# State-space set-up in two parts, one plain pair, and complex products in three passes, in a Trainium2 encoder block

## The chip, the core and the metric

The kernel runs on one core of one Trainium2 chip. Five engines work side by side: PE (TensorE, matrix products; PEld is its weight load), DVE (VectorE), ACT (ScalarE), POOL (GpSimd) and SP (SyncE, which here issues nearly all DMAs, in one queue and in order). Each engine runs its own instructions in order and waits on semaphores of the others. The metric is the time of one execution in microseconds (us), the median of several runs. Arithmetic is float32; a matrix product is built of three matmuls, since each operand is split into a high and a low fp32r part (high x high, high x low, low x high).

## The reference, cut to what matters

```python
h = rms_norm(x, g_ffn1_pre)
x = x + 0.5 * rms_norm(swiglu(h, w_gate, w_up, w_down), g_ffn1_post)   # FFN 1
z = rms_norm(x, g_mix_pre) @ w_in             # -> u | q_c | kv_c | k_rope
y_ssm = rms_norm(s5_mixer(u, fwd, bwd, d_skip, w_glu, b_glu), g_ssm_out)
y_att = rms_norm(mla_mixer(q_c, kv_c, k_rope, ...), g_att_out)
x = x + rms_norm(concat(y_ssm, y_att) @ w_out, g_mix_post)
x = x + 0.5 * rms_norm(swiglu(rms_norm(x, g_ffn2_pre), ...), g_ffn2_post)   # FFN 2

def ssm_direction(u_c, lam_re, lam_im, log_dt, b_re, b_im, c_re, c_im, reverse):
    lam = complex(lam_re, lam_im); dt = exp(log_dt)
    lam_bar = exp(lam * dt)                        # 32 groups x 64 states
    b_bar = ((lam_bar - 1) / lam) * b              # 64 states x 16 channels
    s = linear_recurrence(lam_bar, b_bar @ u_c)    # forwards or backwards in time
    return real(c @ s)
```

x is 512 + 256 = 768 tokens of 1024 channels, D_FF is 2816, there are 32 groups of 16 channels and 8 heads. One layer is computed.

## The kernel before

The stages follow one another on PE: FFN 1, its **way out** (post-norm, residual, pre-norm and transposes into the operand of the next stage), the **mixer** (state-space part and attention), its way out, FFN 2, its way out.

**The FFN** (`ffn`, both times the same function) goes over D_FF in 11 **pairs** of 128 columns, and over the tokens in halves of 384. A **plain** pair takes gate and up as 16 products of 12 matmuls of 128x384; a **Winograd** pair (`wino`) takes 14 such products and some additions of weights on DVE, and needs the combinations T1 to T4 of the activations. T1 to T4 are built once by `combos`, beside the down product of the last plain pair. The down product of a pair (`down`) is 12 products of six matmuls of 128x512, added into `acc` on DVE. Each weight tile is loaded by SP, cast on ACT (line 98) and its remainder taken on DVE (line 99). FFN 1 is called with n_plain = 3 and FFN 2 with n_plain = 1: line 1186 passes 3 for FFN 1, and FFN 2 (the call below it) passes 1. FFN 2 has nothing in the background.

**The state-space set-up** (`ssm_setup`) computes from the parameters alone what the mixer needs: the powers of lam_bar, and for 16 blocks of two groups the matrices W (discretised b times powers) and CL (c times powers). Each complex product is six real passes (`cmul`, lines 517 to 522): W on POOL with 128x256 elements a pass, CL on DVE with 128x320. Per block PE transposes W (`ps_m`, line 668), takes the eight small matmuls of the local kernel (`ps_k`, line 682), and SP writes dM, dO and dK to DRAM (lines 671, 673, 690). The generator is woven into FFN 1 by `behind(steps, PACE)`: after each half product it takes PACE steps of it and ties what these issue behind the last traced instruction of each engine. At `q == n_plain - 1` the rest of it is drained, ahead of `combos`, so the whole of the set-up lies in the three plain pairs.

**The mixer** (`mix`): projection of u; inputs of the state recurrence (`ps_x` from dM, copied into XS); then the **recurrence** on POOL, 62 steps of four dependent instructions each (lines 782 to 785); beside it on PE the projections of q, kv, rope (`rot`, lines 871 and 876) and of the heads. The rotated parts of q go through 16 DMAs into qT (line 878). Attention begins with `ps_s` (line 948). When the recurrence has ended, ACT reverses one direction (line 1017), and `ps_y` (line 1030) takes XS, dO and dK (as T).

**What sets the order.** The code is traced, and a list scheduler then sets the order of each engine from a modelled timeline, the traced order and these ties. Tiles come from pools by tag, with N6 = 18 slots for the wide s6, N4 = 15 for w4 (weights) and N2 = 4 for t2; a tile waits until its slot is free.

## Time and profile before

| what | us |
|---|---|
| median of 3 runs (1502.71 to 1505.95) | 1504.83 |
| the profiled execution | 1503.25 |
| its span | 1501.5 |
| FFN 1, first product to the last | 18.51 to 569.06 |
| of it plain pairs 0 to 2 with the down products and combos | to 254.56 |
| way out of FFN 1 | 569.06 to 616.5 |
| mixer, with its way out | to 976.19 |
| of it recurrence on POOL | 695.77 to 818.69 |
| FFN 2, first product to the last | 976.19 to 1459.35 |

The stages are cut by the first and last matmul of a kind on PE in the trace. PE is busy for 95% of the span; the mean granted clock of PE is 0.979 of full speed. The execution had one core, whose span is the time but for 1.75 us around it.

### The profile page before, as it was taken

Reading aid. Unit: us, or ns where it says so; the run is one execution under the profiler, and the core shown is the slowest. Engines: PE = TensorE matmul, PEld = TensorE weight load, DVE = VectorE, ACT = ScalarE, POOL = GpSimd, SP = SyncE. Lnnn points to the kernel's source line nnn. Section 1 sums busy time; section 2 is a strip of 40 time slices with the busy share of each in tenths; the row PEclk is TensorE's granted clock in tenths of the full one; section 3 lists DMA queues with packets and bytes.
Section 4 is the critical chain, followed back from the end, with each engine's and each line's share of the span. In section 5 each row is a group of like instructions: output and inputs, shape, how many; then the busy total and the mean of one; then the engine's idle time right before and its main releaser. Section 6 shows DMA issues by size and latency. Waiting matters only on the chain. (4 is left out here: it accounts for less than half of the span.)

```text
span 1501.5 us, 20634 instructions
## 1 busy us (share of the span) xinstructions
PE 1427.0 (95%) x7868; PEld 1304.6 (87%) x7868; DVE 1004.7 (67%) x1616; ACT 580.1 (39%) x1101; POOL 347.7 (23%) x525
## 2 busy tenths in 40 slices
PE   6988979999999999899998999799999999999996
PEld 6977858999999997799976988598999999999995
DVE  5596898677766676714265445797777667776664
ACT  5233333233322243424765654346343223332231
POOL 1368740000000003305997112532000000000004
PEclk9999999999999999899999999999999999999999
DMA  8323312212121224462104433322122212212124
GB/s 243 83 73 124 123 60 82 74 58 83 57 84 57 71 87 138 142 191 85 42 1 128 139 100 141 126 99 85 57 71 71 84 57 71 71 57 84 58 97 112
DMA packets 116355, 137.53 MB, mean 92 GB/s; under 512 B 32032, under 2 KB 96928, under 8 KB 116256
## 3 DMA queue, kind: packets, MB, share of 16 engines
q1 hardware_dynamic: 116256, 136.21, 29.7%
q8 instruction: 62, 1.02, 0.3%
q14 instruction: 37, 0.30, 0.1%
HBM read 113.44 MB, written 21.95 MB: 90 GB/s over the span
## 5 line engine op out<-in xcount | busy, mean ns | idle before, releaser
L98 ACT CAST w<-raw 128x512 fp32r<-128x512 f32 (+3 forms) x327 | 219.9, 692 | 297.2 <-PE ps_d L126 88.0
L99 DVE TENSOR_TENSOR w<-raw,w 128x512 fp32r<-128x512 f32 (+3 forms) x327 | 256.0, 799 | 61.2 <-ACT w L98 53.0
L453 DVE TENSOR_TENSOR acc<-acc,ps_d 128x512 f32<-128x512 f32 x216 | 145.9, 683 | 119.2 <-PE ps_d L127 119.0
L125 PE MATMUL ps_d<-w,hid 128*128 128x512 f32 x528 | 210.3, 399 | 7.0 <-DVE acc L453 4.4
L126 PE MATMUL ps_d<-w,hid 128*128 128x512 f32 x528 | 209.5, 397 | 0.0
L127 PE MATMUL ps_d<-w,hid 128*128 128x512 f32 x528 | 207.1, 396 | 0.0
L1146 POOL TENSOR_SCALAR g<-g 128x1024 f32<-128x1024 f32 x2 | 5.6, 2780 | 754.5 <-DMA g<-in_g_ffn_post 419.5
L125 PEld LDWEIGHTS ps_d<-w,hid 128*128 128x128 f32 x528 | 100.3, 190 | 27.2 <-DVE acc L453 5.3
L127 PEld LDWEIGHTS ps_d<-w,hid 128*128 128x128 f32 x528 | 100.4, 190 | 21.8
L126 PEld LDWEIGHTS ps_d<-w,hid 128*128 128x128 f32 x528 | 100.5, 190 | 16.9
L400 ACT COPY U<-pa 128x384 f32<-128x384 f32 x36 | 17.3, 480 | 151.7 <-PE pa L119 143.8
L98 ACT CAST hid<-hs 128x384 fp32r<-128x384 f32 x88 | 44.4, 512 | 74.6 <-DVE hs L348 73.8
L99 DVE TENSOR_TENSOR hid<-hs,hid 128x384 fp32r<-128x384 f32 x88 | 47.9, 557 | 5.4 <-ACT hid L98 5.3
L117 PE MATMUL pe<-T1h,w 128*128 128x384 f32 x144 | 48.8, 339 | 1.8 <-DVE acc L453 1.8
L951 DVE TENSOR_REDUCE mx<-ps_s 128x1 f32<-128x512 f32 (+1 forms) x40 | 27.2, 686 | 32.8 <-PE ps_s L948 32.7
L119 PE MATMUL pe<-T1h,w 128*128 128x384 f32 x144 | 48.9, 339 | 0.0
L118 PE MATMUL pe<-T1l,w 128*128 128x384 f32 x144 | 48.8, 339 | 0.0
L344 ACT ACTIVATE hs<-hs 128x384 f32<-128x384 f32 x54 | 28.3, 526 | 52.1 <-DVE hs L430 39.3
L119 PE MATMUL pa<-B00h,w 128*128 128x384 f32 x144 | 48.4, 336 | 0.0
L117 PE MATMUL pe<-B11h,w 128*128 128x384 f32 x144 | 48.3, 336 | 0.0
L118 PE MATMUL pa<-B00l,w 128*128 128x384 f32 x144 | 48.3, 335 | 0.0
L119 PE MATMUL pe<-B11h,w 128*128 128x384 f32 x144 | 48.3, 335 | 0.0
(372 smaller groups left out, 3893.9 us busy)
## 6 DMA issues: line engine op xcount, KB each, us to landing
raw<-in_w_ffn_gate SPq DMA_DIRECT2D x44, 512.0 KB, 3.7
raw<-in_w_ffn_up SPq DMA_DIRECT2D x44, 512.0 KB, 4.1
raw<-in_w_ffn_down SPq DMA_DIRECT2D x44, 512.0 KB, 3.6
x<-in_x_prompt SPq DMA_DIRECT2D x16, 256.0 KB, 7.4
dO<-ssm_w SPq DMA_DIRECT2D x32, 128.0 KB, 2.1
dM<-ssm_stg SPq DMA_DIRECT2D x16, 256.0 KB, 2.1
raw<-dM SPq DMA_DIRECT2D x8, 512.0 KB, 7.0
raw<-dO SPq DMA_DIRECT2D x8, 512.0 KB, 3.8
```

The source lines that it names most:

```text
L98: self.nc.scalar.copy(hi, src)
L99: (eng or self.nc.vector).tensor_tensor(lo, src, hi.bitcast(F32), op=ALU.subtract)
L117: self.nc.tensor.matmul(ps, A[0][:, k, :], B[0][:, k, :], start=first, stop=False, skip_group_check=True)
L118: self.nc.tensor.matmul(ps, A[0][:, k, :], B[1][:, k, :], start=False, stop=False, skip_group_check=True)
L119: self.nc.tensor.matmul(ps, A[1][:, k, :], B[0][:, k, :], start=False, stop=stop and k == 3, skip_group_check=True)
L125: self.nc.tensor.matmul(ps, lh, rh, start=i == 0, stop=False)
L126: self.nc.tensor.matmul(ps, lh, rl, start=False, stop=False)
L127: self.nc.tensor.matmul(ps, ll, rh, start=False, stop=last)
L344: nc.scalar.activation(hs[:, i, half(nh)], ps, AF.Silu)
L400: nc.scalar.copy(U2, pa)
L453: tt(acc[:, t, sl], acc[:, t, sl], ps, op=ALU.add)
L951: nc.vector.tensor_reduce(m, ps, axis=AX.X, op=ALU.max)
```

## The change

1. FFN 1 is called with n_plain = 1 in place of 3: pairs 1 and 2 become Winograd pairs, and `combos` runs beside the down product of pair 0.
2. `ssm_setup` computes only the front part: powers, W, `ps_m`, dM. It goes behind the halves of pair 0 with 2.0 steps each and behind the down products of pairs 1 to 10 with 0.3 steps each, and is drained ahead of the last two pairs' down product. Two small results go to DRAM, dB (discretised b) and dP (powers).
3. A new `ssm_back` computes CL, `ps_k`, dO and dK in the mixer. It loads dP and, per block, a piece of dB. It is woven behind the projections of q and kv (KPACE = 1.1 steps) and of rope and heads (2.2 steps), and is drained ahead of the first load of dK.
4. Complex products are three passes on DVE (`product`): the two halves of one operand stand side by side, with the signs already in the other operand, so that a pass covers real and imaginary part: 128x512 elements for W, 128x576 for CL. POOL makes none any more.
5. N6 becomes 20 and N2 becomes 6; a scratch size for DMA descriptors is set to 1024.

The diff, cut to its core:

```diff
-PACE = 1.9
+PACE = (2.0, 0.3)
+KPACE = 1.1
...
-    N6, N4, N2 = 18, 15, 4
+    N6, N4, N2 = 20, 15, 6
...
                         if q or nh:
-                            self.behind(background, PACE)
+                            self.behind(background, PACE[0])
...
                 for dh in range(2):
                     product(t, dh, self.dn)()
                     if side is background:
-                        self.behind(side, PACE)
+                        self.behind(side, PACE[1])
...
                 if q == n_plain - 1:
-                    for _ in background:
-                        pass
                     self.free = True
...
                 load_m("u", q + 1)
+        for _ in background:
+            pass
         acc, product = row_of([Q - 1, Q])
...
+        W = {}
+        for b in range(17):
+            if b < 16:
+                W[b] = self.t2("ssm_w", [512])
+                self.product(W[b], self.t2("ssm_t", [512]), Bm, QW, 2 * b, 8)
+                yield
+            if b:
+                ps, w = self.bg([128, 4, 128], "ps_m"), W.pop(b - 1)
+                for x in range(4):
+                    nc.tensor.transpose(ps[:, x, :], w[:, 128 * x : 128 * x + 128], self.ident)
+                stg = self.t2("ssm_stg", [4, 128])
+                nc.scalar.copy(stg, ps)
+                dma(self.dM[:, 2 * b - 2 : 2 * b].rearrange("p g r n -> p (g r) n"), stg)
+                yield
+
+    def product(self, out, tmp, a, b, g0, n):
+        tt = self.nc.vector.tensor_tensor
+        wide = [128, 4, n, 16]
+        a = a[:, g0 : g0 + 2].rearrange("p g r c -> p (g r) c")[:, :, None, :].broadcast_to(wide)
+        b0, b1 = (z[:, g0 : g0 + 2].rearrange("p g r i -> p (g r) i")[:, :, :, None].broadcast_to(wide) for z in b)
+        to = lambda z: z.rearrange("p (x i c) -> p x i c", x=4, c=16)
+        tt(to(out), a, b0, op=ALU.mult)
+        tt(tmp.rearrange("p (g r n) -> p g r n", g=2, r=2)[:, :, ::-1, :], a, b1, op=ALU.mult)
+        tt(out, out, tmp, op=ALU.add)
...
         def matrices(b):
...
+            t = self.s6("ssm_w", [1488])
...
+            dma(v["fB"], self.dB[:, :, 32 * b : 32 * b + 48])
+            self.product(t[:, :576], t[:, 576:1152], CT, PX, 2 * b, 9)
             return v
...
+        back = self.ssm_back()
...
         for nh in range(2):
             for i in range(3):
                 from_h(w_q[i], i, nh, q_done)
+                self.behind(back, KPACE)
...
             proj(wq, slice(512 + 128 * x, 640 + 128 * x), qcT, turned)
+            self.behind(back, 2 * KPACE)
             steps(1)
...
+        for _ in back:
+            pass
 
         kf = self.dK.rearrange("(g q) x -> g q x", q=32)
...
-            way = self.ffn(bl1, (...), out1, 3, feed(), 1, self.ssm_setup(), read)
+            way = self.ffn(bl1, (...), out1, 1, feed(), 1, self.ssm_setup(), read)
```

**SP in FFN 1, the first weight loads after the start.** L69 (L70 after) loads weights (`raw`, of gate, up and down), L671, L673 and L690 write dM, dO and dK from the staging tiles; after, L638 and L649 write dB and dP, L663 dM. Before:

```order
L69 DMA raw<-in_w_ffn_down 128x1024 x2
L673 DMA dO<-ssm_w 128x2x128 x2
L671 DMA dM<-ssm_stg 128x512
L690 DMA dK<-ssm_w 64x240
L671 DMA dM<-ssm_stg 128x512
L673 DMA dO<-ssm_w 128x2x128 x2
L69 DMA raw<-in_w_ffn_gate 128x4x256
L690 DMA dK<-ssm_w 64x240
L673 DMA dO<-ssm_w 128x2x128 x2
L671 DMA dM<-ssm_stg 128x512
L690 DMA dK<-ssm_w 64x240
L671 DMA dM<-ssm_stg 128x512
```

After:

```order
L70 DMA raw<-in_w_ffn_down 128x1024 x2
L70 DMA raw<-in_w_ffn_gate 128x4x256 x2
L638 DMA dB<-ssm_b 128x1056
L649 DMA dP<-ssm_d 128x1152
L663 DMA dM<-ssm_stg 128x512
L70 DMA raw<-in_w_ffn_up 128x4x256 x2
L70 DMA raw<-in_w_ffn_down 128x1024 x2
L70 DMA raw<-in_w_ffn_gate 128x4x256 x2
L663 DMA dM<-ssm_stg 128x512 x2
L70 DMA raw<-in_w_ffn_up 128x4x256 x2
L70 DMA raw<-in_w_ffn_down 128x1024 x2
L70 DMA raw<-in_w_ffn_gate 128x4x256 x2
```

Before, single gate loads stand among the writes of the blocks; after, the loads stand in sixes in the order gate, up, down, with dB, dP and one or two writes of dM between them.

**DVE in the mixer, around the rope products.** L833 to L836 make the latent kv and the rotated key, L841 and L99 split operands, L871 (L913 after) forms the products `rot`; after, L673, L675 and L676 are the three passes of a CL product, L727 and L730 finish a local kernel. Before:

```order
L871 TENSOR_TENSOR rot<-ps,raw 128x384 x2
L833 SCALAR_TENSOR_TENSOR kv<-ps_kv,r,g_kv 128x256
L834 TENSOR_TENSOR kpe<-ps_kv,ropek 128x32
L835 TENSOR_TENSOR kv<-ps_kv,ropek 128x32
L99 TENSOR_TENSOR w<-raw,w 128x8x2x64
L841 TENSOR_TENSOR kvT<-ps_t,kvT 128x128
L871 TENSOR_TENSOR rot<-ps,raw 128x384
L836 TENSOR_TENSOR kpe<-kpe,kv 128x32
L871 TENSOR_TENSOR rot<-ps,raw 128x384
L841 TENSOR_TENSOR kvT<-ps_t,kvT 128x128
L871 TENSOR_TENSOR rot<-ps,raw 128x384 x4
```

After:

```order
L882 TENSOR_TENSOR kvT<-ps_t,kvT 128x128 x2
L673 TENSOR_TENSOR ssm_w<-ssm_b,ssm_d 128x576
L675 TENSOR_TENSOR ssm_w<-ssm_b,ssm_d 128x2x2x144
L727 SCALAR_TENSOR_TENSOR ssm_w<-mask,dsk,ssm_w 64x16
L676 TENSOR_TENSOR ssm_w<-ssm_w 128x576
L730 TENSOR_TENSOR ssm_w<-ssm_w,ps_k 64x16
L913 TENSOR_TENSOR rot<-ps,raw 128x384 x6
L673 TENSOR_TENSOR ssm_w<-ssm_b,ssm_d 128x576
L675 TENSOR_TENSOR ssm_w<-ssm_b,ssm_d 128x2x2x144
L673 TENSOR_TENSOR ssm_w<-ssm_b,ssm_d 128x576
L675 TENSOR_TENSOR ssm_w<-ssm_b,ssm_d 128x2x2x144
L913 TENSOR_TENSOR rot<-ps,raw 128x384 x2
L673 TENSOR_TENSOR ssm_w<-ssm_b,ssm_d 128x576
```

Of the 48 passes of CL, 8 stand ahead of the last copy into XS, and 40 behind it; 26 of these 40 stand ahead of the last `rot<-ps`, 14 behind it.

**POOL in the mixer, around the rotation.** `rec_a`, `rec_b` and XS are the steps of the recurrence, `r` and `rq` norm factors. Before:

```order
L782 TENSOR_TENSOR rec_a<-XS,lam_74 128x128
L783 TENSOR_TENSOR rec_b<-XS,lam_74 128x128
L784 TENSOR_TENSOR rec_a<-rec_a,XS 128x128
L876 TENSOR_TENSOR rot<-rot 128x768 x2
L785 TENSOR_TENSOR XS<-rec_a,rec_b 128x64x2
L170 TENSOR_TENSOR rq<-rq,mhalf 128x6
```

After:

```order
L823 TENSOR_TENSOR rec_b<-XS,lam_76 128x128
L155 TENSOR_TENSOR r<-r,mhalf 128x1
L824 TENSOR_TENSOR rec_a<-rec_a,XS 128x128
L919 TENSOR_TENSOR rot<-rot 128x768
L825 TENSOR_TENSOR XS<-rec_a,rec_b 128x64x2
L822 TENSOR_TENSOR rec_a<-XS,lam_76 128x128
L823 TENSOR_TENSOR rec_b<-XS,lam_76 128x128
L919 TENSOR_TENSOR rot<-rot 128x768
L824 TENSOR_TENSOR rec_a<-rec_a,XS 128x128
```

Both `rot<-rot`, on which the DMAs into qT hang, stood together in the 11th step of the recurrence; they stand now in the 25th and the 26th. On PE, all 16 groups of eight `ps_k` (of which the trace has two records each) stand after the change between `ps_x` and the first `ps_s`; of the 16 groups of four `ps_m`, 9 stand ahead of the last product of FFN 1's gate and up, and 7 in its last down products.

## Rows read from the trace of the kernel before

**Rows 1.** The page: the span, and the busy time of each engine.

```profile
span 1501.5 us, 20634 instructions
PE 1427.0 (95%) x7868; PEld 1304.6 (87%) x7868; DVE 1004.7 (67%) x1616; ACT 580.1 (39%) x1101; POOL 347.7 (23%) x525
```

**Rows 2.** Stretches: us, then PE, PEld, DVE, ACT, POOL busy (count), clock, DMA share, GB/s.

```profile
18.50:569.06 550.56, 530.39 (x2933) 485.91 (x2933) 414.25 (x702) 185.99 (x343) 120.58 (x127) 0.98 0.29 87
18.50:57.80 39.30, 38.80 (x219) 38.00 (x219) 22.58 (x40) 19.31 (x35) 7.64 (x7) 1.00 0.64 167
57.80:254.56 196.76, 177.09 (x1051) 152.26 (x1049) 165.12 (x289) 59.21 (x120) 110.16 (x119) 0.94 0.29 91
300.32:346.08 45.76, 45.76 (x241) 42.68 (x241) 32.65 (x55) 14.70 (x26) 0.00 (x0) 1.00 0.22 69
976.19:1012.90 36.71, 36.71 (x210) 36.64 (x209) 34.48 (x33) 15.25 (x26) 13.41 (x9) 0.95 0.30 101
976.19:1459.35 483.16, 480.89 (x2548) 451.92 (x2547) 354.08 (x548) 174.95 (x302) 24.00 (x12) 1.00 0.23 75
569.06:616.50 47.44, 38.54 (x167) 31.11 (x167) 32.98 (x32) 14.54 (x27) 22.26 (x23) 0.91 0.38 118
```

**Rows 3.** PE timeline in a Winograd pair (start, us): first matmuls of two products.

```profile
302.40 0.33 PE L117 MATMUL pc<-T3h,w 128*128 128x384 f32 x1
...
304.48 0.33 PE L117 MATMUL pd<-T4h,w 128*128 128x384 f32 x1
```

**Rows 4.** Groups by line and form, PE, 18.5 to 569.06: busy us, mean ns, idle before.

```profile
L682 PE MATMUL ps_k<-ssm_w 64*32 64x128 f32 x256 | 19.3, 296 | 10.8 <-DVE ssm_w L689 5.9 <-ACT ssm_stg L670 4.5 <-ACT ssm_w L685 0.4
L668 PE MATMUL ps_m<-ident,ssm_w 128*128 128x128 f32 x64 | 11.6, 311 | 2.4 <-DVE ssm_w L689 2.4
```

**Rows 5.** Groups by line and form, DVE, 18.5 to 569.06: busy us, mean ns, idle before.

```profile
L99 DVE TENSOR_TENSOR w<-raw,w 128x512 fp32r<-128x512 f32 x121 | 84.2, 714 | 17.9 <-ACT w L98 16.9
```

**Rows 6.** Waits of DVE: us in total, times, longest us.

```profile
DVE s L395 <- DMA raw<-in_w_ffn_up: 22.0, 15, 2.4
```

**Rows 7.** Stretches of the mixer, columns as in rows 2.

```profile
690.00:732.00 42.00, 42.00 (x289) 41.83 (x288) 17.85 (x55) 18.51 (x50) 36.93 (x68) 1.00 0.26 74
732.00:750.40 18.40, 17.64 (x93) 15.74 (x92) 0.00 (x0) 16.83 (x31) 16.99 (x37) 1.00 0.13 27
750.40:814.00 63.60, 62.90 (x394) 47.00 (x393) 40.51 (x88) 38.53 (x86) 57.71 (x162) 1.00 0.23 59
```

**Rows 8.** Timeline of all engines in the mixer, 716.9 to 721.

```profile
717.04 0.50 POOL L782 TENSOR_TENSOR rec_a<-XS,lam 128x128 f32<-128x128 f32 x1
...
717.16 1.47 DVE L99 TENSOR_TENSOR w<-raw,w 128x1024 fp32r<-128x1024 f32 x1
...
717.50 1.48 POOL L783 TENSOR_TENSOR rec_b<-XS,lam 128x128 f32<-128x128 f32 x1
...
719.45 0.54 DVE L871 TENSOR_TENSOR rot<-ps,raw 128x384 f32<-128x384 f32 x1
...
719.55 0.47 POOL L785 TENSOR_TENSOR XS<-rec_a,rec_b 128x128 f32<-128x128 f32 x1
```

**Rows 9.** Timeline in FFN 1, DVE and POOL: POOL's pass beside DVE, and alone.

```profile
111.41 0.91 DVE L522 TENSOR_TENSOR ssm_w<-ssm_w,ssm_t 128x320 f32<-128x320 f32 x1
...
111.93 0.86 POOL L517 TENSOR_TENSOR ssm_t<-ssm_q,ssm_a 128x256 f32<-128x256 f32 x1
...
116.41 0.62 POOL L518 TENSOR_TENSOR ssm_w<-ssm_q,ssm_a 128x256 f32<-128x256 f32 x1
```

**Rows 10.** PE timeline: the first scores of attention.

```profile
750.37 1.88 PE L948 MATMUL ps_s<-kT,qT 96*128 96x512 f32 x4
```

**Rows 11.** ACT timeline: the reversal when the recurrence has ended.

```profile
818.72 1.99 ACT L1017 COPY rev<-XS 64x1024 f32<-64x1024 f32 x2 [4.87 <-POOL XS L785]
```

**Rows 12.** PE timeline: the first product that takes the recurrence's states.

```profile
820.80 1.17 PE L1030 MATMUL ps_y<-XS,raw 128*128 128x96 f32 x4 [4.96 <-DVE XS L1019]
```

**Rows 13.** SP timeline: the DMAs of the rotated parts into qT.

```profile
726.29 11.39 SPq L878 DMA_DIRECT2D qT<-rot  x16
```

More of the change, by code (lines that the diff above doesn't have):

```diff
@@ L624, in ssm_setup @@
-        for x in range(2):
-            nc.vector.memset(PX[x], 0.0)
-            nc.vector.tensor_copy(PX[x][0:64, :, 0:9].rearrange("p g i -> p i g"), PW[0:64, x])
-            nc.vector.tensor_copy(PX[x][64:128, :, 1:10].rearrange("p g i -> p i g"), PW[64:128, x, ::-1, :])
-        yield
+        for h, order in ((slice(0, 64), slice(None, None, -1)), (slice(64, 128), slice(None))):
+            for r in range(2):
+                for x, sign in ((0, 1.0), (1, 2.0 * r - 1)):
+                    ts(QW[x][h, :, r, :].rearrange("p g i -> p i g"), q[x][h, order, :], sign, None, op0=ALU.mult)
@@ new lines, in ssm_setup @@
+        yield
+        tB, tD = self.s6("ssm_b", [2, 528]), self.s6("ssm_d", [1152])
+        fx = new("fx", 4).rearrange("p (x r) g -> p x g r", x=2)
+        for r in range(2):
+            ts(fx[:, 0, :, r], fr, 1.0, None, op0=ALU.mult)
+            ts(fx[:, 1, :, r], fi, 2.0 * r - 1, None, op0=ALU.mult)
+        fB, fT = (z.rearrange("p r (g c) -> p g r c", c=16) for z in (tB[:, :, :512], tD[:, :1024].rearrange("p (r x) -> p r x", r=2)))
+        spread = [fx[:, x, :, :, None].broadcast_to([128, 32, 2, 16]) for x in range(2)]
@@ new lines, in ssm_setup @@
+        nc.vector.memset(tB[:, :, 512:], 0.0)
+        tt(fB, Bm, spread[0], op=ALU.mult)
+        tt(fT[:, :, ::-1, :], Bm, spread[1], op=ALU.mult)
+        tt(fB, fB, fT, op=ALU.add)
+        dma(self.dB, tB)
+        yield
+        tD = self.s6("ssm_d", [1152])
+        PX = [tD[:, 576 * x : 576 * x + 576].rearrange("p (g r i) -> p g r i", g=32, r=2) for x in range(2)]
+        for x in range(2):
+            for r in range(2):
+                sign = -1.0 if x and r else 1.0
+                ts(PX[x][0:64, :, r, :].rearrange("p g i -> p i g"), PW[0:64, x], sign, None, op0=ALU.mult)
+                ts(PX[x][64:128, :, r, :].rearrange("p g i -> p i g"), PW[64:128, x, ::-1, :], sign, None, op0=ALU.mult)
+            yield
@@ L632, in ssm_setup @@
                 dma(craw[:, ri, :, s], A[f"c_{p}_{d}"][0].rearrange("(b g) c p -> (g c) b p", b=4))
-            ps = self.bg([128, 4, 128], "ps_c")
-            for b in range(4):
-                nc.tensor.transpose(ps[:, b, :], craw[:, ri, b, :], self.ident)
-            nc.scalar.copy(CT[:, ri], ps.rearrange("p b x -> p (b x)"))
         dsk = self.small.tile([64, 16], F32, name="dsk")
@@ L663, in inputs @@
-        def inputs(v):
-            g0 = 2 * v["b"]
-            ps = self.bg([128, 2, 2, 128], "ps_m")
-            for g in range(2):
-                for x in range(2):
-                    nc.tensor.transpose(ps[:, g, x, :], v["W"][:, x, 128 * g : 128 * g + 128], self.ident)
-            stg = self.t2("ssm_stg", [2, 2, 128])
-            nc.scalar.copy(stg, ps)
-            dma(self.dM[:, g0 : g0 + 2], stg)
-            for x in range(2):
-                dma(self.dO[:, g0 : g0 + 2, x, :], v["CL"][:, x, :, 1:9, :].rearrange("p g i c -> p g (i c)"))
+        for ri in range(2):
+            ps = self.bg([128, 4, 128], "ps_c")
+            for b in range(4):
+                nc.tensor.transpose(ps[:, b, :], craw[:, ri, b, :], self.ident)
+            nc.scalar.copy(CT[:, :, ri, :], ps.rearrange("p b (g c) -> p (b g) c", c=16))
@@ L692, in ssm_setup @@
         ready = []
-        for b in range(18):
+        for b in range(17):
             if b < 16:
                 ready.append(matrices(b))
-            yield
-            if b >= 2:
+            if b:
                 v = ready.pop(0)
-                inputs(v)
-                yield
+                outputs(v)
                 kernels(v, 0)
@@ L841, in mix @@
                 tt(kvT[x][:, 1, tok(t)], pt[:, x, :], kvT[x][:, 0, tok(t)].bitcast(F32), op=ALU.subtract)
+            self.behind(back, KPACE)
             steps(1)
@@ L887, in mix @@
             proj(wq, slice(128 * p, 128 * p + 128), qcT, two_heads(qT[p]))
+            self.behind(back, 2 * KPACE)
             steps(1)
```

64 lines of the change are left out of this document (31 added, 33 removed).

## The prediction, made before the changed kernel was run

> **What bounds the kernel now.** I read the page first: PE is busy for 95% of the span [rows 1], so a change can only bring what PE does not do, what it does slowly, or what others make it wait for. Then the table of stretches, stage by stage, because an average over stages hides that. In FFN 1 PE is busy 530.39 of 550.56 us; of the 20.2 us of idle time 19.7 lie between 57.8 and 254.56, in the two plain pairs that carry the set-up, where the clock is 0.94 too and POOL and DVE work for 110 and 165 us [rows 2]. A Winograd pair behind them takes 45.76 us with PE busy throughout at clock 1.00, DVE at 32.65 us [rows 2]. FFN 2 is the same function with one plain pair and no background: 483.16 us, against 550.56 for FFN 1 [rows 2]. So this kernel has already run FFN 1's new program, without the set-up, in 67.4 us less.
>
> The mixer is bound twice. PE is full until attention starts at 750.37 and through attention [rows 7, 10]. POOL's recurrence, begun at 695.77, ends only after it: ACT waits 4.87 us for the last XS and takes it at 818.72, and PE idles 4.96 us before the first product with it, at 820.80 [rows 11, 12]. POOL's chain ends last, by 5 us.
>
> **The change part by part.** All sums are made against the profiled execution, 1503.25 us; the median is 1.6 us more.
>
> *FFN 1.* Pairs 1 and 2 have 14 products where they had 16. Twelve matmuls take 304.48 - 302.40 = 2.08 us [rows 3], so two pairs give 4 x 2.08 = 8.3 us. Out of FFN 1 go `ps_k` (128 matmuls, two records each), 19.3 us of PE and 10.8 us of idle time before them [rows 4], and with them the cover of two pairs in which everything waited on everything. I don't add these up: FFN 2's time contains them all. New FFN 1 = 483.16 (rows 2), + 2.6, since pair 0 began more slowly here (39.30 against 36.71, rows 2), + 9 groups of `ps_m` at 11.6/16 = 0.73 us each [rows 4] = 6.6, + about 3 for places where the set-up holds a load or a slot back. That is 495.4, or **-55 us**. The front's DVE work, 16 products of three passes of 128x512, costs 0.71 us a pass [rows 5], 34 us, or 3.4 us a pair, and a pair leaves DVE 13.1 us free [rows 2]: hidden. POOL has nothing in a steady pair, so nothing locks there. The 3 us are a choice. Its bounds: nothing at all, with the `ps_m` falling where PE waits anyway (-65), and 2.4 us for each of ten pairs, DVE's longest wait for a weight of an up half [rows 6], in place of the 3 (-34). I take 3 because in the order the weight loads stand in regular sixes with one or two dM between them, and each dM waits for one ACT copy.
>
> *Way out.* Seven groups of `ps_m` stand in the last down products, where PE has no other wait: 7 x 0.73 = **+5** [rows 4]. Not below 0, and at most this, as PE idles 8.9 us of that stretch later on [rows 2].
>
> *Mixer, PE.* 19.3 us of `ps_k` [rows 4] and 1.2 of `ps_c` come in ahead of attention, where PE is full: attention can't begin before 771, and PE would come to `ps_y` 20.5 us later, 5 of which it waited anyway [rows 12]: +15.5.
>
> *Mixer, POOL.* 40 of CL's 48 passes lie beside the recurrence. DVE has room: 17.85 of 42 us, then nothing for 18.4 us [rows 7]. What they do to POOL is in a row: a DVE pass with two SBUF inputs (`w<-raw`, 128x1024, 1.47 us) makes the POOL instruction issued into it take 1.48 us, where the one before took 0.50; a DVE pass with one input in PSUM (`rot<-ps`) leaves POOL its 0.47 [rows 8]. So 0.98 us lost for 1024 elements, and 0.55 for a pass of 576: 40 x 0.55 = 22 us. The smaller price is in FFN 1, 0.86 against 0.62 beside passes of 320 elements [rows 9]: 0.24, 0.43 at 576, 17 us in all. I take the first, since the row stands in this very loop. Two us more for a later start (8 passes stand ahead of the last copy into XS): the recurrence ends at 842.7 and `ps_y` comes at 844.8, **+24**.
>
> The Trainium skill ("SBUF — State Buffer", Who interferes with whom) says that such a pair excludes each other for the whole instruction, whoever issues first. The trace agrees in rows 8 and not in rows 9, where POOL slowed by 0.24 and did not stop; the rival below has what the rule would make of the time.
>
> *Mixer, attention.* Both `rot<-rot` move from POOL's 11th step to the 25th and 26th, and the qT DMAs behind them. Before, these were issued from 726.29 [rows 13], which lies 24 us ahead of attention. Fifteen steps at 2.05 us (four instructions of about 0.5, rows 8) put the second one at some 757, the lock of 26 passes at 0.55 adds 14: 771, then the last DMAs and their landing, about 778 in place of 750.4. The 63.6 us of attention [rows 7] end near 842. Two chains meet at 842 to 845, so neither's loss adds to the other's: the mixer costs 24. Bounds: 15.5 from PE alone, and 34 by a full lock.
>
> FFN 2 and the two later way-outs have the same instructions as before: 0. N2, N6 and the scratch size: 0; what they let go earlier is in the sum.
>
> Sum: -55 + 5 + 24 = **-26**: 1477.2 for the profiled execution, some 1479 as a median.
>
> **The rivals.**
> 1. *The lock is cheaper than PE.* DVE's passes fall between POOL's instructions; then PE's 15.5 us decide: -55 + 5 + 15.5 = -34.5, 1470. For it: rows 9. Against: rows 8, and the late rotation. Chance 0.18.
> 2. *The lock is whole.* Every pass stops POOL for its own length: 0.71 x 576/512 = 0.80 us [rows 5], 40 of them 32 us, with the 2 us 34: -16, 1489. This is what the rule named above gives. For it: in rows 8, 0.98 of 1.47 us were lost. Against: rows 9. Chance 0.09.
> 3. *The set-up starves the pairs.* SP is one queue: a load behind a dM waits for a copy on ACT, which waits for PE and DVE; and four wide tiles of the set-up hold s6 slots. With 2.4 us lost in each of ten pairs FFN 1 gives 34: -34 + 5 + 24 = -5, 1500. For it: this is how the three plain pairs were slow. Against: of each pair DVE has 13 us and ACT 31 us free [rows 2], and only 1.6 blocks fall on a pair. Chance 0.12, a third of it past the edge of what counts as the same.
> 4. *Slower: the back part becomes a chain.* A block of CL is a DMA of dB, three passes, `ps_k`, an ACT copy, a DVE piece, again ACT, DVE, and dO and dK to DRAM before its `ssm_w` tile is free. All `ps_k` stand on PE ahead of `ps_s`, so the last block holds attention up. With two blocks in flight it is done by 771 and I have counted it. If tiles are so few that one follows another, the 16 blocks take 16 times their chain. The mixer must lose 50 us to undo the rest, which is attention at 805, since PE's wait of 5 us before `ps_y` is there to be filled: from a first block near 683, 7.6 us a block. At 10 us, which the two DMAs of 2 us, three passes of some 1.2 and seven hand-overs may reach, attention starts at 843, +93 less 5: 1543. For it: the order has `ps_k` in one run of 48 matmuls, so blocks do bunch. Against: the same order has passes of two blocks side by side. Chance 0.09.
>
> **How the numbers follow.** Forecast 0.52, rivals 0.18, 0.09, 0.12, 0.09. The likeliest is the forecast: 1479. Two runs' medians of this kernel can tell 0.2%, 3 us, from no change. Faster: 0.52 + 0.18 + 0.09 + two thirds of 0.12 = 0.87; same: the rest of rival 3, 0.04; slower: rival 4, 0.09. The range begins where every term takes its lower end, -65 + 0 + 15.5 = -49.5, or 1455, and ends at rival 3, 1500; rival 4 is left out.
>
> **What would show it.** Right: FFN 1 from the first `ps` to the last `pe` takes about 495 us, with PE busy over 97% and clock 1.00 from pair 1 on; `ps_k` lies between `ps_x` and `ps_s`; the recurrence's 128x128 instructions average well over 525 ns; the wait of ACT for the last XS stands near 842; attention starts near 778, after a wait of PE for qT. Wrong in part: if PE begins attention at 771 without a wait, rival 1; if POOL's instructions take 0.5 + 0.8, rival 2; if DVE waits for `raw` in each pair, with SP waiting on `ssm_stg`, rival 3; if PE waits for `ssm_w` before `ps_k` again and again, rival 4. The forecast falls altogether if FFN 1 takes over 530 us or the mixer loses over 50.

## The result: slower by 4.3%, and the profile after

The changed kernel takes 1569.4 us (median of 4 runs, 1567.71 to 1570.56) against 1504.41 us before: the ratio is 1.0431, 95% interval 1.0413 to 1.0449. The forecast was 1479, faster; the time lies 69 us above the end of the range. The profiled execution took 1570.34 us, 67 more than the one before, with a span of 1568.3 us.

Cut at the same matmuls as the table of the kernel before:

| stretch | before | after | forecast | measured |
|---|---|---|---|---|
| FFN 1, first `ps` to last `pe` | 550.5 | 535.2 | -55 | -15.3 |
| last `pe` to first `ps_x` (way out, u) | 92.2 | 102.4 | +5 | +10.2 |
| first `ps_x` to first `ps_s` | 89.1 | 165.6 | +28 | +76.5 |
| first `ps_s` to the end | 751.1 | 746.3 | -4 | -4.8 |
| span | 1501.5 | 1568.3 | -26 | +66.8 |

(The forecast had +24 for the mixer: attention begins 28 later, at 778 in place of 750.4, and 4 of these are made good behind it, where PE waited for the recurrence.) So FFN 1 brought a good quarter of what was expected, and the mixer cost three times as much, 71.7 us.

The page of the changed kernel first: span and busy times, to be read beside [rows 1].

```profile
span 1568.3 us, 20453 instructions
PE 1440.1 (92%) x7820; PEld 1314.1 (84%) x7820; DVE 1051.2 (67%) x1678; ACT 585.7 (37%) x1117; POOL 287.4 (18%) x413
```

PE's work is the same within 13 us, its share fell from 95 to 92%: the loss is waiting, and with the waiting a lower clock (a mean of 0.954 over the span, 0.979 before). The table of stretches says where (columns as in [rows 2]): FFN 1, one slow Winograd pair of it, way out, from the first `ps_kv` to attention, attention, FFN 2 to its last `pe`.

```profile
18.77:554.00 535.23, 502.71 (x2600) 468.69 (x2599) 397.10 (x669) 181.25 (x318) 36.51 (x14) 0.96 0.25 77
402.95:457.57 54.62, 48.33 (x248) 44.83 (x248) 36.81 (x61) 15.85 (x29) 0.00 (x0) 0.94 0.21 68
554.00:616.00 62.00, 47.55 (x209) 39.04 (x210) 46.30 (x50) 21.44 (x41) 26.32 (x28) 0.89 0.40 128
686.60:822.00 135.40, 94.67 (x632) 80.36 (x631) 66.84 (x134) 41.38 (x110) 120.52 (x235) 0.76 0.29 69
822.00:890.20 68.20, 65.45 (x398) 48.42 (x397) 45.15 (x93) 44.57 (x95) 14.67 (x43) 0.97 0.21 54
```

A Winograd pair took 45.76 us with PE busy throughout [rows 2]; this one takes 54.62, with 6.3 us of idle PE and a clock of 0.94. The stretch of the projections, 60 us before (42.00 and 18.40, PE full, [rows 7]), takes 135.4 us, with 40.7 us of idle PE and a clock of 0.76. The waits of PE (us in total, times, longest) name who was late:

```profile
PE pb L118 <- ACT w L99: 24.4, 6, 6.3
...
PE ps_k L723 <- DMA ssm_w<-dB: 8.3, 4, 2.7
PE ps_t L880 <- DVE kvT L882: 7.3, 2, 6.7
PE ps_t L880 <- DVE kv L874: 6.3, 2, 3.2
PE ps_k L723 <- issue: 5.8, 1, 5.8
PE ps L126 <- DVE rot L913: 5.4, 1, 5.4
...
PE ps_k L723 <- DVE ssm_w L676: 3.4, 1, 3.4
```

The first row is FFN 1: six pairs in which PE waits for a weight, at its product `pb`. The others are the mixer: no single wait, but one after another.

### The profile page after: what moved, and what is told of

It reads as the page before. It is cut to its first block, busy times and chain, and to the rows that moved or that the text cites. A ratio compares the mean times of both kernels' runs of the same rounds, so it can differ in the third digit from the quotient of the medians.

```text
span 1568.3 us, 20453 instructions
## 1 busy us (share of the span) xinstructions
PE 1440.1 (92%) x7820; PEld 1314.1 (84%) x7820; DVE 1051.2 (67%) x1678; ACT 585.7 (37%) x1117; POOL 287.4 (18%) x413
## 5 line engine op out<-in xcount | busy, mean ns | idle before, releaser
L99 ACT CAST w<-raw 128x512 fp32r<-128x512 f32 (+2 forms) x335 | 224.0, 691 | 332.9 <-DVE raw L398 99.1
L100 DVE TENSOR_TENSOR w<-raw,w 128x512 fp32r<-128x512 f32 (+2 forms) x335 | 267.5, 814 | 58.0 <-ACT w L99 55.5
L118 PE MATMUL pb<-T2h,w 128*128 128x384 f32 x160 | 57.8, 361 | 24.4 <-ACT w L99 24.4
L99 ACT CAST hid<-hs 128x384 fp32r<-128x384 f32 x88 | 44.6, 513 | 64.7 <-DVE hs L349 55.9
L119 PE MATMUL pb<-T2l,w 128*128 128x384 f32 x160 | 57.1, 357 | 4.7 <-DVE T2l L273 4.7
L120 PE MATMUL pb<-T2h,w 128*128 128x384 f32 x160 | 57.0, 356 | 0.0
L118 PEld LDWEIGHTS pb<-T2h,w 128*128 128x128 f32 x160 | 32.4, 203 | 27.9 <-ACT w L99 26.9
L118 PE MATMUL pe<-T1h,w 128*128 128x384 f32 x160 | 54.6, 341 | 0.0
L119 PE MATMUL pe<-T1l,w 128*128 128x384 f32 x160 | 54.3, 340 | 0.0
L118 PE MATMUL pa<-B10h,w 128*128 128x384 f32 x160 | 53.9, 337 | 0.0
L119 PE MATMUL pa<-B10l,w 128*128 128x384 f32 x160 | 53.8, 337 | 0.0
```

What stands on the lines that cost most here:

```text
L99: self.nc.scalar.copy(hi, src)
L100: (eng or self.nc.vector).tensor_tensor(lo, src, hi.bitcast(F32), op=ALU.subtract)
L118: self.nc.tensor.matmul(ps, A[0][:, k, :], B[0][:, k, :], start=first, stop=False, skip_group_check=True)
L119: self.nc.tensor.matmul(ps, A[0][:, k, :], B[1][:, k, :], start=False, stop=False, skip_group_check=True)
L120: self.nc.tensor.matmul(ps, A[1][:, k, :], B[0][:, k, :], start=False, stop=stop and k == 3, skip_group_check=True)
```

## FFN 1: which wait holds the pairs

The DVE timeline of a slow pair, up to its wait (start, us; line 454 adds a down product, lines 673 to 676 are a product of the set-up, lines 396 to 398 the additions of weights that a Winograd half needs):

```profile
393.97 0.69 DVE L454 TENSOR_TENSOR acc<-acc,ps_d 128x512 f32<-128x512 f32 x1 [0.67 <-PE ps_d L128]
395.33 0.69 DVE L454 TENSOR_TENSOR acc<-acc,ps_d 128x512 f32<-128x512 f32 x1 [0.67 <-PE ps_d L128]
396.69 0.69 DVE L454 TENSOR_TENSOR acc<-acc,ps_d 128x512 f32<-128x512 f32 x1 [0.67 <-PE ps_d L128]
397.29 0.69 DVE L673 TENSOR_TENSOR ssm_w<-ssm_a 128x512 f32<-128x512 f32 x1
397.89 0.68 DVE L675 TENSOR_TENSOR ssm_t<-ssm_a,ssm_q 128x512 f32<-128x512 f32 x1
398.50 1.29 DVE L396 TENSOR_TENSOR s<-raw 128x512 f32<-128x512 f32 x2
399.70 0.68 DVE L676 TENSOR_TENSOR ssm_w<-ssm_w,ssm_t 128x512 f32<-128x512 f32 x1
400.30 1.28 DVE L397 TENSOR_TENSOR raw<-raw 128x512 f32<-128x512 f32 x2
401.50 0.68 DVE L398 TENSOR_TENSOR raw<-s,raw 128x512 f32<-128x512 f32 x1
402.93 0.69 DVE L100 TENSOR_TENSOR w<-raw,w 128x512 fp32r<-128x512 f32 x1 [0.74 <-ACT w L99]
```

The additions stand behind the last of the twelve `acc`, though DVE waited for PE before each of the last three, and had room there. Three reasons offered themselves: the weights came late because SP's queue held them behind dM (theory Q below); the passes kept DVE busy (rival D); or the additions had no tile (theory T). Their tile `s1` comes from t2, and so do `ssm_w`, `ssm_t` and `ssm_stg`: by the program, `ssm_w` is held until the transposes are done, and `ssm_stg` until the write of dM is.

**dm_act.**

```diff
-                dma(self.dM[:, 2 * b - 2 : 2 * b]..., stg)
+                nc.scalar.dma_start(self.dM[:, 2 * b - 2 : 2 * b]..., stg)
```

> Only the 16 writes of dM in FFN 1 are issued by ACT, behind ACT's own copy, and not by SP. Theory Q (the weight loads of the up half stand in SP's queue behind a dM that waits for PE's transposes and ACT's copy): the gaps of 3 to 6 us before pb in each Winograd pair go, the pairs return to about 46 to 48 us, FFN 1 from its first ps to its last pe takes about 500 us in place of 535, the whole some 1533. Rival D (DVE's set-up passes hold up the additions of weights): FFN 1 stays over 525 and the whole over 1558.

Measured 1568.03 us; FFN 1 took 532.1. The wait is there unchanged:

```profile
PE pb L118 <- ACT w L99: 24.2, 6, 6.2
```

The second load of the up half, with no dM ahead of it in the queue, still goes out 7 us before PE's wait ends (392.46 and 399.58; 395.77 and 402.95 in the changed kernel), for it waits for PE's down product. So a write of dM in SP's queue is not the reason; theory Q, which is also how the prediction's third rival put it, falls.

**s1_own4.**

```diff
-    N6, N4, N2 = 20, 15, 6
+    N6, N4, N2 = 20, 15, 4
...
-            s1 = self.t2("s1", [4, 128])
+            s1 = self.pool.tile([128, 4, 128], F32, tag="s1", name="s1", bufs=2)
```

> The additions' tile s1 of each Winograd half gets two slots of its own, and t2 goes from 6 to 4, the same memory in all; nothing else. Theory T (in the slow pairs s1 waits for a t2 slot that a tile of the set-up holds until its transposes, its copy and its write of dM are done, so DVE's additions of weights stand behind the last acc of the down product, and pb waits): the gaps of 3 to 6 us before pb go, a pair takes 46 to 48 us, FFN 1 takes 495 to 503 us in place of 535, the whole some 1532. Rival D (the passes themselves keep DVE from the additions): FFN 1 stays over 525, the whole over 1558.

The additions get slots of their own, and t2 gives up as many, so that the memory is the same. Measured 1529.96 us, ratio to before 1.0179 (1.0164 to 1.0194): 39 us less than the changed kernel. FFN 1 takes 500.5 us, in the range of theory T. The row of the stretch (columns as above), and DVE's timeline at the corresponding place:

```profile
18.70:519.20 500.50, 491.11 (x2603) 460.69 (x2602) 392.87 (x672) 181.86 (x319) 36.41 (x14) 0.99 0.28 83
```

```profile
367.71 0.69 DVE L454 TENSOR_TENSOR acc<-acc,ps_d 128x512 f32<-128x512 f32 x1 [0.83 <-PE ps_d L128]
370.07 0.69 DVE L396 TENSOR_TENSOR s<-raw 128x512 f32<-128x512 f32 x1 [1.67 <-DMA raw<-in_w_ffn_up]
370.68 0.68 DVE L454 TENSOR_TENSOR acc<-acc,ps_d 128x512 f32<-128x512 f32 x1
371.28 0.68 DVE L673 TENSOR_TENSOR ssm_w<-ssm_a 128x512 f32<-128x512 f32 x1
```

The addition now stands among the `acc`, and `pb <- ACT w` is gone from the waits. The work on DVE is the same (392.87 against 397.10 us), so the passes were hidden, as forecast. This shows that the shared tag made the pairs slow. The edit also changes the order that the scheduler gives DVE and SP, so it does not show which of t2's holders kept `s1` waiting; and t2's 4 slots in place of 6 were not tried without the rest. Of the 34.7 us that FFN 1 gained, 23.1 are idle time of PE (32.5 to 9.4) and 11.6 busy time for the same matmuls (502.71 to 491.11): the clock, a mean of 0.96 with the gaps and 0.99 without.

**plain3** leaves the changed kernel as it is but for the number of plain pairs.

```diff
-... out1, 1, feed(), 1, self.ssm_setup(), read)
+... out1, 3, feed(), 1, self.ssm_setup(), read)
```

> The changed kernel with three plain pairs again: the front part of the set-up then lies behind the halves of the plain pairs, where no s1 is needed; the back part stays in the mixer. Theory T: the Winograd pairs run at 45.8 us without gaps, FFN 1 takes 505 to 520 us in place of 535 though it has 8.3 us more of products, the whole some 1545. Rival (the one plain pair gains its 8.3 us and more): FFN 1 over 535, the whole over 1569.

Measured 1528.73 us, FFN 1 512.5 (row as above):

```profile
19.70:532.30 512.60, 500.94 (x2668) 468.01 (x2667) 377.06 (x634) 176.81 (x308) 37.59 (x14) 1.00 0.28 85
```

Three plain pairs are faster than one here by 41 us, though they hold 8.3 us more of products. FFN 1 has 23 of these: the front part lies beside pairs that need no `s1`, and the Winograd pairs behind take 45.76 us again. Of the rest, 8 are the way out, where no piece of the front part is left, and 11 the stretch to the scores, for which no run has the reason.

## The mixer: what the back part costs, and why

**cl_memset** leaves the three passes of CL out.

```diff
-            self.product(t[:, :576], t[:, 576:1152], CT, PX, 2 * b, 9)
+            nc.vector.memset(t[:, :576], 0.0)
```

> The three passes of each CL product are left out (a memset of the tile stands in their place, so dO and the local kernels are zero); all DMAs, ps_k, copies and the weaving stay. Theory L (DVE's passes and what they take from POOL make the mixer late): attention begins at about 775 in place of 822, the recurrence ends near 817, the whole some 1525. Rival C (the coupling of the queues by the back part's ps_k, copies and DMAs makes it late): attention begins after 800, the whole stays over 1550.

**no_psk** leaves the local kernels out.

```diff
-            ps = self.bg([64, 128], "ps_k")
-            ... (four matmuls)
             if d == 0:
-                nc.scalar.copy(KF[:, 112:240], ps)
-                stt(KF[:, 112:128], mask, dsk[:, b : b + 1], KF[:, 112:128], ...)
+                nc.vector.memset(KF, 0.0)
             else:
-                nc.scalar.copy(KF[:, 0:112], ps[:, 0:112])
-                tt(KF[:, 112:128], KF[:, 112:128], ps[:, 112:128], op=ALU.add)
                 dma(self.dK[64 * b : 64 * b + 64, :], KF)
```

> The changed kernel without the small matmuls ps_k, their copies and the two small DVE instructions behind each (a memset of the tile stands in their place, so the local kernels are zero); the passes, the weaving and all DMAs stay. In the changed kernel the stretch from the first ps_kv to the first scores takes 135 us, 60 before; without the passes it took 104.5. Theory C (ps_k, in PE's order among the projections, makes PE wait for what DVE and SP have not done yet): 75 to 85 us, the whole some 1515. Rival L (the passes alone make it long, through DVE and POOL): 110 or more, the whole over 1540.

Measured 1536.87 and 1538.0 us, 33 and 31 less than the changed kernel. Neither theory stands alone. The rows from the first `ps_kv` to the first scores, of cl_memset and then of no_psk:

```profile
683.70:788.20 104.50, 86.80 (x602) 74.36 (x600) 32.66 (x97) 39.72 (x106) 93.52 (x217) 0.84 0.35 82
```

```profile
679.90:763.60 83.70, 68.00 (x375) 63.73 (x374) 54.14 (x115) 34.38 (x78) 74.89 (x104) 0.88 0.43 101
```

Of the 135.4 us, the passes are worth 31 and `ps_k` with its copies 52; before, the stretch took 60. So in time most is `ps_k`, but the sum of 83 for the two together is more than the 75 there are to explain: each waits for the other. no_psk gave back less in all than its stretch, because attention then began so early that the recurrence, still late by the passes, stood in ACT's way: ACT waited 18.73 us for the last XS with a copy of the attention behind it, and PE waited for that copy (PE's waits, and ACT's timeline).

```profile
PE ps_o L1013 <- ACT PT L978: 21.1, 1, 21.1
```

```profile
830.03 1.99 ACT L1055 COPY rev<-XS 64x1024 f32<-64x1024 f32 x2 [18.73 <-POOL XS L817]
```

The second row answers [rows 11]. The lock itself, DVE and POOL in each other's way, was priced well. From the first `rec_a` to the last XS the recurrence takes 122.9 us before, 139.7 after, and 121.2 without the passes: 18.5 us for the 39 passes that lie beside it in the trace, 0.47 each; forecast 0.55 and 22. Both sides gave. In the groups by line and shape of the changed kernel from 694 to 834, POOL's four instructions of 128x128 are at 565 to 727 ns, where cl_memset has 464 to 554, and DVE's three passes of 128x576 at 850 to 995. The dearest line of either engine, and then POOL's same line in cl_memset (680 to 812):

```profile
L824 POOL TENSOR_TENSOR rec_a<-rec_a,XS 128x128 f32<-128x128 f32 x30 | 21.8, 727 | 0.1
...
L675 DVE TENSOR_TENSOR ssm_w<-ssm_b,ssm_d 128x576 f32<-128x576 f32 x13 | 12.9, 995 | 0.0
```

```profile
L824 POOL TENSOR_TENSOR rec_a<-rec_a,XS 128x128 f32<-128x128 f32 x30 | 16.6, 554 | 0.0
```

But in the changed kernel this lock decided nothing. The recurrence ends at 834.18; ACT comes to the reversal only 21 us later and does not wait (ACT's timeline), and PE takes the first product with the states at 892.80, without a wait where it waited 4.96 us before [rows 12].

```profile
855.08 1.04 ACT L1063 COPY rev<-XS 64x1024 f32<-64x1024 f32 x1
```

**back_dma_act.**

```diff
-            dma(v["fB"], ...)
+            nc.scalar.dma_start(v["fB"], ...)
...
-                dma(self.dO[...], ...)
+                nc.scalar.dma_start(self.dO[...], ...)
...
-                dma(self.dK[...], KF)
+                nc.scalar.dma_start(self.dK[...], KF)
```

> In the mixer the loads of dB and the writes of dO and dK are issued by ACT and not by SP. Theory S (SP's queue holds the mixer up: ropeq, dB and the qT DMAs behind writes that wait): PE's waits for dB (8.3 us) and for ropeq (5.4 us) go, attention begins near 800, the whole some 1548. Rival C (the coupling of PE, DVE and POOL in order does): within 5 us of 1569, or slower, since ACT now waits for DVE at each dO.

Measured 1575.21 us, no better: the waits for dB went, and PE waited 13.0 us for one `kv` instead. Nor did attention wait for the DMAs into qT. The changed kernel issues them from 793.68, though `rot` is done at 771, but the last has landed by 806, and PE works on the projections and `ps_v` until the scores begin at 822.

**back_last** doesn't weave the back part at all (the four calls of `behind(back, ...)` are taken out).

> ssm_back isn't woven behind the projections; all of it is issued where it was drained, after the products of v, and the scheduler places it. Both rotations stand in POOL's 11th step again. Theory W (the weaving puts the back part ahead of what attention needs, on DVE, POOL and SP): attention begins at about 772 to 780 in place of 822, the whole some 1525. Rival (the work itself is too long for the stretch, wherever it stands): attention begins after 800, the whole over 1550.

Measured 1556.45 us, 31 more than theory W said. It is half right: from the first `ps_kv` to the scores 60.9 us pass, as in the kernel before (59.8). But the back part then lies in the attention, which takes 130.8 us in place of 64:

```profile
742.40:873.20 130.80, 102.13 (x662) 69.59 (x662) 89.39 (x173) 52.38 (x129) 85.01 (x172) 0.74 0.31 73
```

The bill only moved.

**early_only and early_b** begin the back part at u, ahead of the recurrence, where DVE has little to do; early_b has s1_own4's edit too.

```diff
+        back = self.ssm_back()
         for i in range(4):
             from_h(w_u[i], i, 1, u_done)
+            self.behind(back, 2)
-        back = self.ssm_back()
...
                 nc.scalar.copy(o[64:128, :, :, 65:96], ps[64:128, :, :, 95:64:-1])
+            self.behind(back, 1)
```

> The back part is begun before the second halves of u: two steps behind each of these four products, one behind each of the eight blocks of ps_x, the rest behind q; 45 of the 48 passes then stand ahead of the last copy into XS, where POOL has no recurrence and DVE is idle for some 40 us. Theory P (the place costs, not the work): attention begins near 775 and ends with the recurrence near 840, the whole some 1522. Rival (the work costs 60 us wherever it stands, since it only moves ahead of the recurrence): ps_x and the recurrence begin 30 us or more later, attention after 800, the whole over 1550.

> Both of the edits above, s1 in slots of its own and the back part begun at u. If the two causes add: some 37 us less in FFN 1 and 47 less in the mixer, about 1485, faster than the kernel before. If one hides the other, or the back part's early loads collide with the way out of FFN 1: over 1510.

Measured 1561.47 and 1516.32 us (early_b: ratio 1.0099, 1.0078 to 1.012). So the early place brings 8 us in the one and 14 in the other, measured against s1_own4, where 47 were expected. In early_b the stretch from the first `ps_kv` to the scores is shorter, 84.2 us in place of 135.4, but from the first `ps_x` to the first `ps_kv` 66.3 us pass, 29.3 before. There ACT waits for a weight that SP issued late, behind dB, dO and dK, and PE for ACT's copies (timelines of ACT and of PE):

```profile
646.10 0.91 ACT L99 CAST w<-raw 128x864 fp32r<-128x864 f32 x1 [12.79 <-DMA raw<-in_w_in]
```

```profile
647.35 2.02 PE L809 MATMUL ps_x<-U,raw 128*128 128x96 f32 x8 [11.53 <-ACT XS L813]
```

That put SP's queue under suspicion again. Four more kernels, all with early_b's edits, take DMAs from it: one load of dB in place of 16 (early_one), then dO and dK issued by POOL (early2_one_pool, three steps behind each u), by ACT (early_one_act), or by POOL and the start one half earlier (earlier_one_pool).

> As early_b (1516), but dB is loaded once into one tile at the start of the back part, so 16 loads of a block's piece leave SP's queue; dO and dK stay on SP. If SP's queue is what cost early_b its expected gain (w_in was issued behind dB, dO and dK, ACT waited for it, and PE waited 11.5 us for ACT's copies of XS): some 1505. If the order of ps_k among ps_x on PE does it: within 4 us of 1516.

> As early_one, and dO and dK are issued by POOL, which is idle until the recurrence; three steps behind each of the u products in place of two, so that all 48 passes stand ahead of the recurrence. Theory S (SP's queue): no wait over 5 us of PE between ps_x and ps_kv, the recurrence begins near 665, attention near 735, the whole some 1485, faster than the kernel before. Rival (PE's order, or POOL now holds the blocks up by its own DMAs): over 1505.

> As early_one with dO and dK issued by ACT, whose copies of XS and casts of weights then stand behind writes that wait for DVE. If any queue that is taken from SP is enough: as the run on POOL, some 1490. If a busy engine that waits for DVE at each block is as bad as SP: over 1510.

> As the run with POOL, and the back part is begun one half earlier still: one step behind each first-half product of u, beside the way out of FFN 1, where PE waits anyway. If the back part only needs an uncrowded place: some 1480. If its loads and DVE passes collide with the way out (DVE does the norms there): the first ps_x comes 10 us or more later than 617 and the whole stays over 1500.

Measured 1523.99, 1510.11, 1523.41 (two runs 15 us apart) and 1508.65 us. Fewer loads on SP gain nothing over early_b. The two with POOL are 6 and 8 us under early_b; they also begin with other numbers of steps, so what POOL's queue has of it is not shown. None reaches the time that its edit was to bring (1505, 1485, 1490 and 1480). In early2_one_pool all passes stand ahead of the recurrence and take 750 ns each, with no lock, and still the stretch of `ps_x` takes 69.6 us, PE at a clock of 0.66 (the stretch, then groups of DVE by line and shape from 590 to 700):

```profile
622.40:692.00 69.60, 57.13 (x411) 45.66 (x412) 41.30 (x88) 23.12 (x70) 25.23 (x41) 0.66 0.44 106
```

```profile
L673 DVE TENSOR_TENSOR ssm_w<-ssm_b,ssm_d 128x576 f32<-128x576 f32 x16 | 12.0, 750 | 14.8 <-DMA raw<-dM 14.8
L731 DVE TENSOR_TENSOR ssm_w<-ssm_w,ps_k 64x16 f32<-64x16 f32 x16 | 2.6, 163 | 15.0 <-ACT ssm_w L730 14.6
```

Each of the sixteen blocks passes from DVE to PE, and then twice from PE to ACT to DVE, in a stretch in which `ps_x` too passes from PE to ACT and DVE. Measured from the last `pe` of FFN 1 to the end, against 932.4 us before, the set-up costs 82 us in the changed kernel, 68 in back_last, 62 in early_b and 54 and 52 in the two with POOL (in each 6 to 14 of these are the way out). That the hand-overs from engine to engine are what costs is the reading that is left; how these 52 us divide among them, no run has separated.

## The set-up in FFN 1, and a version faster than both

**whole3 and whole2** put the back part behind the front part in FFN 1, with three and two plain pairs, all drained ahead of `combos`.

```diff
                 yield
+        yield from self.ssm_back()
...
-        back = self.ssm_back()
+        back = iter(())
...
                 if q == n_plain - 1:
+                    for _ in background:
+                        pass
```

> The changed kernel with three plain pairs and with the back part put behind the front part in FFN 1, both drained ahead of combos, 1.5 steps behind each half product: of the change there remain the three passes on DVE, the new layouts and the slots; the mixer has no set-up. If the mixer's loss comes from the back part alone, the mixer takes 181 us from the last pe to the first scores again and the rest 750, as in the kernel before, and FFN 1, which was 512.5 with the front part alone, takes 512.5 + 20.5 of PE for ps_k and ps_c + some 7 of waits = 540: the whole some 1490, faster than the kernel before. Rival (six passes on two engines were no slower than three on one, POOL's share being free there): FFN 1 takes 550 or more and the whole 1503 or more.

> As the run with the whole set-up in FFN 1, but with two plain pairs and 2.6 steps behind each half. If PE's work bounds the plain pairs: 4 us less, some 1486. If the chain of DVE, PE and SP in the set-up does: one plain pair less to cover it, and its 45 us come out as waits of PE: FFN 1 some 560, the whole over 1505.

**whole3_sb** also keeps b and the powers in their tiles (no dB, no dP).

> As the run with the whole set-up in the three plain pairs of FFN 1 (1509.8), but the discretised b and the powers stay in their tiles: no dB, no dP, no loads of them. There PE waited 12.7 us for ssm_w <- dB in the plain pairs, which had a clock of 0.91. If these round trips through DRAM, which the split in two parts needs, are what made it slower than the kernel before: 12.7 us less and some of the clock back, 1490 to 1497. If DVE's passes bound that stretch whatever feeds them: over 1503.

Measured 1509.79, 1517.72 and 1508.38 us (whole3_sb: ratio 1.0036, 1.0022 to 1.0049). With the set-up out of it the mixer is as before (whole3: 183.8 us from the last `pe` to the scores, before 181.3). FFN 1 is not: 557.5, 566.0 and 556.3. Three passes on one engine are no gain here: DVE got no less to do in the plain pairs. The six CL passes took DVE 69.1 us before (12.6, 12.1, 11.6, 11.2, 11.0 and 10.6 by line); W's and CL's three take it 71.8, since POOL's share came over. Nor are the round trips through DRAM the cause: without dB's loads the time is the same within its interval, and PE waits 14.1 us for `ssm_w` of DVE in place of 12.7 for dB (a row of PE's waits of whole3, and of whole3_sb):

```profile
PE ps_k L726 <- DMA ssm_w<-dB: 12.7, 7, 2.2
```

```profile
PE ps_k L724 <- DVE ssm_w L731: 14.1, 4, 9.9
```

**rev3 and rev2** turn the split round. CL, `ps_k`, dO and dK, which need wide tiles, lie in three or two plain pairs; W, `ps_m` and dM, which need t2 alone, behind the Winograd pairs; `s1` has its own slots, b and the powers stay in their tiles. The paces change with it (1.5 and 0.35 steps in rev3, 2.6 and 0.33 in rev2). The core of the edit:

```diff
+        yield from self.ssm_back()
+        self.plain_done = True
         W = {}
         for b in range(17):
...
                 if q == n_plain - 1:
+                    while not self.plain_done:
+                        next(background)
```

> The split the other way round: CL, ps_k, dO and dK (with the discretised b kept in its tile) lie in three plain pairs of FFN 1, where wide tiles are free; W, ps_m and dM, which need only t2 tiles, lie behind the Winograd pairs, with s1 in slots of its own; the mixer has no set-up. What the runs so far price: CL's part costs FFN 1 some 45 us in plain pairs when W lies there too (557.5 against 512.5), W's part some 15 behind Winograd pairs (500.5 against 485.8), and the mixer is as before. If CL's part takes less with the plain pairs for itself, 25 to 35: FFN 1 some 535, the whole some 1490, faster than both kernels. If it takes its 45 there too: FFN 1 some 550, the whole 1503 or more.

> The same with two plain pairs and 2.6 steps behind each half: 4 us of products less, and one pair less for CL's blocks. If CL's chain (three passes, ps_k, two copies and two small instructions, some 3 us a block) fits beside one pair and a half: some 1486. If not, what is left comes out before combos as waits of PE: over 1500.

Measured 1483.53 us, ratio to the kernel before 0.988 (0.9866 to 0.9894), and 1493.56 us, 0.9931 (0.9918 to 0.9943). rev3 is faster than both kernels. Its stretches: FFN 1, the plain pairs, a piece of the length of a Winograd pair, and `ps_x` to the scores.

```profile
19.70:548.90 529.20, 517.34 (x2930) 475.07 (x2930) 410.16 (x715) 183.96 (x342) 33.35 (x15) 0.99 0.31 88
57.80:254.00 196.20, 185.09 (x1133) 162.41 (x1132) 164.02 (x309) 64.01 (x129) 22.75 (x7) 0.98 0.28 77
254.00:299.76 45.76, 45.76 (x245) 42.60 (x244) 34.78 (x59) 15.27 (x27) 0.00 (x0) 1.00 0.23 74
642.50:732.00 89.50, 88.72 (x588) 86.33 (x588) 30.98 (x80) 53.71 (x124) 55.38 (x105) 1.00 0.26 68
```

The second row answers the 196.76 us of [rows 2], whose clock was 0.94: the stretch is no shorter, but by 254 it has done more of the Winograd work. The third row shows PE full at a clock of 1.00 while W is made; from one pair's `pb` to the next pair's, 46.6 to 47.1 us pass in most of these pairs, against 45.76 without W. The mixer's 89.5 us are before's 89.1. So the back part has no fixed price. FFN 1 with the front part alone, s1_own4's 500.5, and 8.3 for two more plain pairs, would be 508.8, an estimate; rev3's 529.2 is 20 us more, which is what the prediction counted as PE's own work for `ps_k` and `ps_c` (20.5). The same blocks cost 52 us and more behind FFN 1, beside work with hand-overs of its own. Which of rev3's edits has what share of the 21 us that it gains over the kernel before was not tried.

## Why the prediction was wrong, point by point

- *What bounds the kernel.* Right: the plain pairs with the set-up were the slow place of FFN 1, and FFN 2's program is nearly to be had there, at 500.5 us with 495.4 forecast, once its tiles are left to it (s1_own4).
- *FFN 1, "about 3 for places where the set-up holds a load or a slot back".* This term was mis-sized: it measured 43 (535.2 less 492.4), with 12 of them clock. Its upper bound came from a wait for a DMA [rows 6]; what was short was a slot, in t2, and I had looked at SP's order and at s6. DVE's order could have shown it: in FFN 2 the additions stand among the `acc`, in FFN 1 after the change behind them. I compared the loads' rows and not DVE's.
- *Rival 3* (the set-up starves the pairs, 1500, chance 0.12) had the place right, and its queue and its tiles wrong; its price of 24 us was too small.
- *Way out.* +10.2 against +5: five groups of `ps_m` come behind the last `pe` in the trace, not seven, but the last products of W lie there on DVE too, which is busy for 46.30 us of 62, and the forecast had counted PE alone.
- *Mixer, POOL.* Right in kind and nearly in size: 18.5 us of lock against 22, 0.47 us a pass, between the 0.43 worked out from rows 9 and the 0.55 from rows 8. But the forecast took its +24 from this chain, as the one that ends last, and there it failed: the recurrence was over 59 us before PE's first product with its states. The Trainium skill's whole exclusion ("SBUF — State Buffer", Who interferes with whom) would have made the lock 32, at 0.80 a pass; this case does not bear that out.
- *Mixer, PE: "+15.5".* This is the step that failed most. 20.5 us of PE's work were counted as if PE would find its operands ready. PE's order has `ps_k` among the projections, and each waits for a pass, a piece of dB, or an ACT copy that stands behind another of PE's products; 40.7 us of idle time and a clock of 0.76 came of it, and the first `ps_x` to the scores took 165.6 us where 117 were forecast. "Two chains meet at 842 to 845, so neither's loss adds to the other's" was wrong in the same way: what DVE does for the passes and what PE, ACT and DVE do for `ps_k` both lay on PE's chain, 31 and 52 us of it when taken out one at a time. No wait of PE for qT came, either.
- *Rival 4* (a chain of blocks, 1543, chance 0.09) came nearest. It asked for 7.6 us a block to lose what FFN 1 gained; from the first pass at 685.2 to the last `ps_k` at 801.5 it was 7.3. The mixer lost 72 us even so, not some 50, since projections and `ps_v`, 20 us of them, still stood behind the last `ps_k` on PE. Its sign, PE waiting for `ssm_w` before `ps_k` again and again, is in the rows, and so are both things by which the forecast was to fall: FFN 1 over 530 us, the mixer's loss over 50. Its cause, too few `ssm_w` tiles, was not tried; its argument against, that passes of two blocks stand side by side, says nothing about waits.
- *FFN 2 and the rest: 0.* Right for FFN 2, 483.3 us against 483.16. The -4.8 from the scores to the end is a sum: PE's wait of 4.96 us for the recurrence is gone [rows 12], the attention took 4 us longer, and what follows it 4 us less, for which no run has the reason.
- The range left rival 4 out, and what two wrong terms make together. FFN 1's term was bounded by a wait of the trace before, the mixer's by PE's work and POOL's lock: neither bound had anything of the kind that came.

## What to carry to other kernels

A tile tag that foreground and background share is a queue like any other: before weaving work behind a tight loop, list which of the loop's tiles come from a tag that the new work holds across a DMA. Work moved "beside" a stage is to be priced by its hand-overs between engines in order, and not only by the busy time that it adds: here PE was full in the stage and the other engines had time, and still there was no room for a chain that returned to PE for each of sixteen blocks. And look at which memory each half of a divided job needs: in rev3 the half that needs no wide tiles went behind the loop that has none to spare.

## What the runs showed of the hardware

The granted clock is part of the price of a wait. In FFN 1, 23 us of idle time, most of it in six waits of up to 6.3 us, cost another 12 through a mean granted clock of 0.96 in place of 0.99 (the changed kernel and s1_own4). It shows behind the wait that ends at 402.95: matmuls of 128x384 follow each other at 0.32 us at first, the lower level of 1.2 GHz, and then again at 0.17, that of 2.4 GHz. From `ps_kv` to the scores, where PE kept idling, the mean was 0.76, and 0.66 in the stretch of `ps_x` in early2_one_pool. And where a DVE pass with two SBUF inputs meets POOL, both lose: the pass of 128x576 went from 750 ns (early2_one_pool) to 850 to 995 in the changed kernel, and each cost POOL 0.47 us.
